# Hybrid encoder trunk on one core: the whole program scheduled on the framework's detailed timing simulator instead of its simple one

## The chip, the cores and the metric

The kernel runs on one core of one Trainium2 chip. The metric is the device time of one execution in microseconds (us). The core's engines are TensorE (PE: matmuls, with weight loads listed as PEld), VectorE (DVE), ScalarE (ACT), GpSimd (POOL) and SyncE (SP, whose queue issues all transfers of this kernel). Each engine takes its instructions from a queue of its own, and semaphores tie the queues together.

## The reference

A residual stream x of 512 positions by 1024 channels, in float32, passes one even and one odd layer and a final RMSNorm:

```python
def even_layer(x, ...):
    u = rms_norm(x, norm_g) @ w_in
    q_c, kv_c, k_r, z_b, glu_a, glu_g, z_a = jnp.split(u, ...)
    o_b = mla(q_c, kv_c, k_r, w_uq, q_g, w_ukv, kv_g, cos, sin) * jax.nn.silu(z_b)
    o_a = conformer_conv(glu_a, glu_g, conv_w, conv_b, ln_g, ln_b) * jax.nn.silu(z_a)
    return x + (jnp.concatenate([o_b, o_a], axis=-1) @ w_out).astype(x.dtype)

def odd_layer(x, ...):
    u = rms_norm(x, norm_g) @ w_in
    z_c, xbc, dt_f, dt_b, g_b, g_c, h_d, z_d = jnp.split(u, ...)
    o_c = ssd_mixer(z_c, xbc, dt_f, dt_b, ...)
    o_d = short_conv(g_b, g_c, h_d, conv_d_w) * jax.nn.silu(z_d)
    return x + (jnp.concatenate([o_c, o_d], axis=-1) @ w_out).astype(x.dtype)
```

`mla` is full attention with 16 heads over 512 positions, on low-rank queries and keys. `conformer_conv` is a gated input, a depthwise convolution of width 31, a layer norm over the channels and a swish. `ssd_mixer` is a state-space scan in chunks of 128 positions, in both directions, with 24 heads in 4 groups, behind a depthwise convolution of width 5 and followed by a gated, grouped norm. `short_conv` is a gated depthwise convolution of width 3.

## The kernel before

**Matmuls and weights.** Each float32 product is split into a high and a low part (fp32r) and made as three matmuls: high x high, high x low, low x high. A weight slab is transferred to a raw tile (two buffers), cast to `w_hi` on ScalarE (L87) and reduced to its remainder `w_lo` (L88), on VectorE for early slabs and every second one of the output projections, otherwise on GpSimd; `w_hi` and `w_lo` have three buffers each. `mm_cm` (L318) makes one tile of 128 channels by 512 positions with 24 matmuls into one bank; `mm_tm` (L345) makes four tiles with positions on the partitions. PSUM has eight banks by tag: acc 3, cv 1, sb 2, tp 2.

**Even layer.** Normed input (L405 to L407), the low-rank inputs, then eight pairs of heads. For each pair and each block of 128 queries the scores go into an sb bank (L529), VectorE takes their maximum `mx` (L531), ScalarE the exponential `p` (L533). The blocks of p are transposed on TensorE (L266) into a tp bank, copied out (L556), and multiplied with the values (L566). Scores of the block after next need the sb bank that the exponential has released. Projections (L318) for the gates and the convolution's input stand in between. In program order the width 31 convolution comes behind all eight pairs: per tile of 128 channels, ScalarE starts it in the cv bank (L470), VectorE adds 22 taps (L481), GpSimd the others on the side (L478 to L484). Behind it come the layer norm's statistics (L632 to L640, result `rs2`) and their broadcast over the partitions by a small matmul (L273, two results in the two sb banks). The output projection `oe` (L345) takes the attention's tiles, split into `o_s` pages, as its first four slabs, and calls `conformer` ahead of the fifth:

```python
def conformer():
    for ct in range(8):
        th, v, y = page("ln_th", "att"), page("ln_v", "att"), u[ct]
        V.tensor_tensor(y, y, lb[0], op=ALU.mult)                # L649
        V.tensor_tensor(y, y, lb[1], op=ALU.subtract)            # L650
        SC.activation(th, y, AF.Tanh, ...)                       # L651
        SC.activation(v, y, AF.Identity, ...)                    # L652
        V.scalar_tensor_tensor(v, th, 1.0, v, ...)               # L653
        G.tensor_tensor(oT[8 + ct], oT[8 + ct], v, op=ALU.mult)  # L654
    for o, p in zip((oh, ol), split_pages(oT[8:], None, (big("o_hi"), big("o_lo")))):
        o.extend(p)                                              # L360 o_hi, L361 o_lo
```

`split_pages` casts to `o_hi` on ScalarE (L360) and takes the remainder `o_lo` on GpSimd for each third tile, the first among them, and on VectorE for the others (L361).

**Odd layer.** For each group of heads, channel tiles are projected (L318), convolved with width 5 (ScalarE L718, four taps on VectorE L720, a tanh on ScalarE, the product on VectorE L722; the tiles are named c, c5, BT and CT) and transposed into an sb bank (L266). The scan's pairs of heads make decay factors on ScalarE and VectorE (L898 to L907, results e and f), the products within a chunk (L910, cv bank), the state's share (L862 to L868, St; L926, L931 to L936, xs), and the norm (L946 to L950). Projections of the next group's tiles are handed in between as work to fill. The output projection `oo` (L345) and the final norm end the program.

**What sets the order.** Nothing in the kernel says what stands where in a queue. The program is written as a sequence of calls, and the framework's tile context schedules it: it simulates the engines, and at each simulated moment lets an engine take, of the operations whose inputs and buffers are ready, the one that is earliest in program order. The order in which the operations were taken becomes the order of the queue. Buffers of a tag are handed out in the same walk. So the convolutions, late in program order but ready early, serve as fill on VectorE and GpSimd beside the attention pairs.

Of the kernel before, what the change touches and what calls it, by code (L numbers as in the profile page):

```python
# [1072 lines left out]
def _program(arrays, dbg=None):  # L1073
    import concourse.bacc as bacc

    nc = bacc.Bacc("TRN2", target_bir_lowering=False, num_devices=1)
    A = {n: nc.dram_tensor("in_" + n, a.shape, mybir.dt.from_np(a.dtype), kind="ExternalInput").ap()
         for n, a in arrays.items()}
    out = nc.dram_tensor("out", (S, D), F32, kind="ExternalOutput").ap()
    with tile.TileContext(nc) as tc, ExitStack() as ctx:  # L1080
        trunk(ctx, tc, A, out, dbg)
    return nc

# [8 lines left out]
```

## Time and profile before

| | us |
|---|---|
| time, median of 3 runs | 990.68 (989.94 to 990.91) |
| the profiled execution | 989.05 |
| its span in the trace | 987.2 |
| TensorE busy / VectorE busy in the span | 929.5 / 737.1 |
| ScalarE busy / GpSimd busy | 464.8 / 385.2 |
| mean granted TensorE clock | 0.983 of full speed |

The span is the time from the first to the last instruction of the profiled execution. The stages follow one another: input and low-rank projections to about 60 us, the attention pairs with the convolutions to about 400, the Conformer's tail and the output projection to about 500, the odd layer's inputs to about 600, the state-space groups to about 890, the last output projection and norm to the end. A line of a view names the source line, the engine, the operation and its tiles (result<-inputs). Idle time stands with what ended it.

### The profile page before, as it was taken

The numbers are of one execution on the slowest core, as the hardware profiler recorded it, in microseconds if no ns is written. First come the engines' busy times: TensorE is split into PE (matmuls) and PEld (weight loads), VectorE is DVE, ScalarE is ACT, GpSimd is POOL, SyncE is SP. The second block draws the span as 40 slices with busy tenths as digits, with TensorE's granted clock in tenths as the row PEclk, the third lists the DMA queues.
The fourth block names the chain that finished last, engine by engine and source line by source line (L and its number), as shares of the span: only waits on it lengthen the run. The fifth ranks groups of instructions, "written<-read, shape, count | busy, mean of one in ns | idle before, by whom it ended". The sixth has DMA issues, their size and how long they took to land. (4 is left out here: it accounts for less than half of the span.)

```text
span 987.2 us, 12582 instructions
## 1 busy us (share of the span) xinstructions
PE 929.5 (94%) x4564; PEld 754.8 (76%) x4564; DVE 737.1 (75%) x1295; ACT 464.8 (47%) x916; POOL 385.2 (39%) x272
## 2 busy tenths in 40 slices
PE   7899999999999999999999999888878988999996
PEld 7887686686786777888899987766756876787885
DVE  4799888899898998952357457899898968956205
ACT  6646444454444544543242546455456555434312
POOL 0251734526337063461143454334423443445221
PEclk9999999999999999999999999999889999999999
DMA  8313312212212126233343533432332423322222
GB/s 307 102 30 112 56 54 66 70 25 102 70 25 96 52 69 168 71 112 107 123 142 89 172 110 104 106 86 86 107 107 88 124 89 103 111 101 90 87 86 86
DMA packets 42326, 95.99 MB, mean 97 GB/s; under 512 B 12136, under 2 KB 13800, under 8 KB 42264
## 3 DMA queue, kind: packets, MB, share of 16 engines
q1 hardware_dynamic: 42264, 95.19, 31.2%
q8 instruction: 36, 0.59, 0.2%
q14 instruction: 26, 0.21, 0.1%
HBM read 90.85 MB, written 4.33 MB: 96 GB/s over the span
## 5 line engine op out<-in xcount | busy, mean ns | idle before, releaser
L88 POOL TENSOR_TENSOR w_lo<-w_raw,w_hi 128x1024 fp32r<-128x1024 f32 (+2 forms) x68 | 160.4, 2361 | 254.2 <-ACT w_hi L87 155.1
L87 ACT CAST w_hi<-w_raw 128x1024 fp32r<-128x1024 f32 (+7 forms) x142 | 135.0, 952 | 202.9 <-PE acc L318 58.7
L318 PE MATMUL acc<-xT_hi,w_hi 128*128 128x512 f32 x544 | 223.1, 412 | 2.7 <-ACT xT_hi L406 2.7
L318 PE MATMUL acc<-xT_lo,w_hi 128*128 128x512 f32 x544 | 220.9, 407 | 0.0
L88 DVE TENSOR_TENSOR w_lo<-w_raw,w_hi 128x1024 fp32r<-128x1024 f32 (+6 forms) x74 | 83.8, 1132 | 96.8 <-ACT w_hi L87 92.5
L318 PE MATMUL acc<-xT_hi,w_lo 128*128 128x512 f32 x544 | 144.7, 400 | 0.0
L481 DVE SCALAR_TENSOR_TENSOR cv<-u,pc,cv 128x497 f32<-128x497 f32 (+10 forms) x176 | 130.2, 740 | 10.0 <-ACT cv L470 7.7
L318 PEld LDWEIGHTS acc<-xT_hi,w_hi 128*128 128x128 f32 x544 | 106.0, 195 | 25.6 <-ACT xT_hi L406 2.9
L318 PEld LDWEIGHTS acc<-xT_lo,w_hi 128*128 128x128 f32 x544 | 105.6, 194 | 22.4 <-POOL xT_lo L407 0.4
L318 PEld LDWEIGHTS acc<-xT_hi,w_lo 128*128 128x128 f32 x544 | 103.3, 192 | 21.3
L479 POOL TENSOR_TENSOR side<-side 128x510 f32<-128x510 f32 (+3 forms) x56 | 78.5, 1402 | 4.7
L484 POOL TENSOR_TENSOR u<-cs,side 128x512 f32<-128x512 f32 x8 | 11.0, 1374 | 157.1 <-issue 149.9
L533 ACT ACTIVATE p<-sb,mx 128x512 f32<-128x512 f32 x64 | 43.4, 684 | 20.9 <-DVE mx L531 20.6
L904 DVE SCALAR_TENSOR_TENSOR e<-e,nacs 128x128 f32<-128x128 f32 x96 | 45.9, 520 | 9.6 <-ACT e L903 9.6
L478 POOL TENSOR_SCALAR side<-u,pc 128x510 f32<-128x510 f32 (+3 forms) x56 | 50.2, 897 | 4.7
L899 DVE SCALAR_TENSOR_TENSOR f<-cbm,dt,f 128x128 f32<-128x128 f32 x96 | 47.4, 538 | 0.4 <-ACT f L898 0.4
L531 DVE TENSOR_REDUCE mx<-sb 128x1 f32<-128x512 f32 x64 | 41.7, 685 | 3.2 <-PE sb L529 2.4
L903 ACT ACTIVATE e<-e,nacs 128x128 f32<-128x128 f32 x96 | 31.4, 391 | 22.1 <-DMA e<-acs 18.9
L720 DVE SCALAR_TENSOR_TENSOR c<-acc,pc,c 128x510 f32<-128x510 f32 (+1 forms) x48 | 35.7, 743 | 7.7 <-ACT c L718 7.4
L266 PEld LDWEIGHTS tp<-kc,p 128*128 128x128 f32 x256 | 28.9, 140 | 16.0 <-ACT pt L556 10.7
L529 PE MATMUL sb<-k_t,qk_hi 128*128 128x512 f32 (+1 forms) x128 | 39.6, 404 | 0.5 <-DVE k_t L257 0.4
L566 PE MATMUL acc<-pt,v_tm 128*64 128x512 f32 x128 | 37.6, 608 | 1.5 <-DVE pt L556 1.5
(336 smaller groups left out, 1918.5 us busy)
## 6 DMA issues: line engine op xcount, KB each, us to landing
w_raw<-in_w_cm_o SPq DMA_DIRECT2D x36, 512.0 KB, 3.5
w_raw<-in_w_cm_e SPq DMA_DIRECT2D x32, 512.0 KB, 3.6
e<-acs SPq DMA_DIRECT2D x24, 512.0 KB, 5.2
w_raw<-in_w_out_e SPq DMA_DIRECT2D x16, 512.0 KB, 3.5
w_raw<-in_w_out_o SPq DMA_DIRECT2D x16, 512.0 KB, 3.5
w_raw<-in_w_z SPq DMA_DIRECT2D x12, 384.0 KB, 3.2
xt<-in_xT SPq DMA_DIRECT2D x8, 256.0 KB, 5.2
x_t<-in_x SPq DMA_DIRECT2D x4, 512.0 KB, 6.9
```

Source lines behind the costliest of these rows:

```text
L87: nc.scalar.copy(hi, raw)
L88: eng.tensor_tensor(lo, raw, hi.bitcast(F32), op=ALU.subtract)
L318: T.matmul(a, l, r, start=n == 0, stop=n == 3 * kk - 1)
L478: G.tensor_scalar(t[:, o], ut[:, i], wt(j), 0.0, op0=ALU.mult, op1=ALU.add)
L479: G.tensor_tensor(side[:, o], side[:, o], t[:, o], op=ALU.add)
L481: V.scalar_tensor_tensor(c[:, o], ut[:, i], wt(j), c[:, o], op0=ALU.mult, op1=ALU.add)
L529: T.matmul(s, l[:, qs], r, start=n == 0, stop=n == 2)
L531: V.tensor_reduce(mx, s, axis=AX.X, op=ALU.max, negate=True)
L533: SC.activation(p, s, AF.Exp, bias=mx, accum_out=sums[:, q:q + 1])
L566: T.matmul(o[j * HD:(j + 1) * HD], v_tm[:, k, (h0 + j) * HD:(h0 + j + 1) * HD], pt, start=k == 0, stop=k == NT - 1, skip_group_check=True)
L899: V.scalar_tensor_tensor(f[:, cc], cbm[1][:, cc], dt[:, c, hb:hb + 1], f[:, cc], op0=ALU.mult, op1=ALU.add)
L904: V.scalar_tensor_tensor(e[:, cc], rb[:, 1, cc], nacs[:, c, hb:hb + 1], e[:, cc], op0=ALU.add, op1=ALU.min)
```

## The change

One argument is added where the tile context is made. The scheduler then takes its simulated moments from the framework's detailed timing simulator and no longer from the simple one:

```diff
-    with tile.TileContext(nc) as tc, ExitStack() as ctx:
+    with tile.TileContext(nc, schedule_with_timeline_sim=True) as tc, ExitStack() as ctx:
         trunk(ctx, tc, A, out, dbg)
```

The operations are the same in number and kind, and so are pools, tags and buffer counts; 370 of 1654 tiles get another buffer of their tag. On TensorE 3134 of 4278 instructions stand at another place (132 later to 51 earlier), on VectorE 1096 of 1295, on ScalarE 665 of 803, on GpSimd 80 of 274 (at most 9 places), on SP 85 of 231 (at most 7). Three places follow; a tile's number is that of its allocation.

**VectorE, from the first to the second pair of heads.** mx_1146 is the first maximum of the second pair, cv_3384 and cv_3428 are the second and third tile of the convolution, oT_1091 is the first pair's output. Before:

```order
L617 TENSOR_TENSOR oT_1091<-acc_1094,oT_1091 128x512
L481 SCALAR_TENSOR_TENSOR cv_3384<-u_735,pc_81,cv_3384 128x506
L257 TENSOR_TENSOR qk_lo_1139<-tp_1133,qk_hi_1138 96x512
L589 TENSOR_TENSOR oT_1091<-oT_1091,inv_947 128x512
L531 TENSOR_REDUCE mx_1146<-sb_1142 128x1
L531 TENSOR_REDUCE mx_1154<-sb_1150 128x1
L88 TENSOR_TENSOR w_lo_1272<-w_raw_1269,w_hi_1271 128x1024
L531 TENSOR_REDUCE mx_1162<-sb_1158 128x1
```

Now, the same maxima:

```order
L617 TENSOR_TENSOR oT_1091<-acc_1094,oT_1091 128x512
L257 TENSOR_TENSOR qk_lo_1139<-tp_1133,qk_hi_1138 96x512
L481 SCALAR_TENSOR_TENSOR cv_3428<-u_1029,pc_81,cv_3428 128x504
L589 TENSOR_TENSOR oT_1091<-oT_1091,inv_947 128x512
L481 SCALAR_TENSOR_TENSOR cv_3428<-u_1029,pc_81,cv_3428 128x505
L481 SCALAR_TENSOR_TENSOR cv_3428<-u_1029,pc_81,cv_3428 128x506
L481 SCALAR_TENSOR_TENSOR cv_3428<-u_1029,pc_81,cv_3428 128x507 x2
L481 SCALAR_TENSOR_TENSOR cv_3428<-u_1029,pc_81,cv_3428 128x506
L531 TENSOR_REDUCE mx_1146<-sb_1142 128x1
L531 TENSOR_REDUCE mx_1154<-sb_1150 128x1
```

The taps of the third tile, which stood behind the second pair before, stand ahead of its first maximum. Between the first maximum of the first pair and mx_1146 there are 39 taps, where there were 15.

**TensorE and GpSimd, the join of the Conformer.** sb_3866 and sb_3871 are the two broadcasts of the layer norm's factors (L273), acc_3882 and acc_3916 gate projections, w_hi_3992 and w_hi_4022 the third and fourth slab of the output projection, w_hi_4052 the fifth, the first that takes the Conformer's tiles. TensorE before:

```order
L318 MATMUL acc_3882<-xT_hi_435,w_lo_3729 128x512 x7
L273 MATMUL sb_3866<-kc_80,rs2_3845 128x128 x4
L273 MATMUL sb_3871<-kc_80,rs2_3845 128x128 x4
L318 MATMUL acc_3882<-xT_hi_435,w_lo_3729 128x512
L318 MATMUL acc_3916<-xT_hi_435,w_hi_3878 128x512
L318 MATMUL acc_3916<-xT_lo_436,w_hi_3878 128x512
```

TensorE now, first the broadcasts, then the start of the fifth slab:

```order
L345 MATMUL acc_3958<-w_hi_3992,o_s_3776 128x512
L345 MATMUL acc_3958<-w_hi_3992,o_s_3777 128x512
L273 MATMUL sb_3866<-kc_80,rs2_3845 128x128 x4
L273 MATMUL sb_3871<-kc_80,rs2_3845 128x128 x4
L345 MATMUL acc_3958<-w_hi_3992,o_s_3780 128x512
L345 MATMUL acc_3958<-w_hi_3992,o_s_3781 128x512
L345 MATMUL acc_3958<-w_lo_3993,o_s_3776 128x512
L345 MATMUL acc_3958<-w_lo_3993,o_s_3780 128x512
L345 MATMUL cv_3959<-w_hi_3992,o_s_3776 128x512
```

```order
L345 MATMUL cv_3959<-w_lo_4023,o_s_3784 128x512
L345 MATMUL cv_3959<-w_lo_4023,o_s_3788 128x512
L345 MATMUL acc_3956<-w_hi_4052,o_hi_4144 128x512
L345 MATMUL acc_3957<-w_hi_4052,o_hi_4144 128x512
L345 MATMUL acc_3958<-w_hi_4052,o_hi_4144 128x512
L345 MATMUL cv_3959<-w_hi_4052,o_hi_4144 128x512
L345 MATMUL acc_3956<-w_hi_4052,o_lo_4145 128x512
```

The broadcasts stood ahead of the last gate projection and of all four o_s slabs; they stand in the middle of the third of them now, 87 matmuls later, with 34 matmuls between them and the first on o_hi. On GpSimd, the difference (- before, + now) at the products L654 of the same tiles:

```order
+L88 TENSOR_TENSOR w_lo_4053<-w_raw_4050,w_hi_4052 128x1024
 L654 TENSOR_TENSOR oT_2944<-oT_2944,ln_v_4081 128x512
-L88 TENSOR_TENSOR w_lo_3993<-w_raw_3990,w_hi_3992 128x1024
 L654 TENSOR_TENSOR oT_2978<-oT_2978,ln_v_4089 128x512
+L88 TENSOR_TENSOR w_lo_4195<-w_raw_4192,w_hi_4194 128x1024
 L654 TENSOR_TENSOR oT_3202<-oT_3202,ln_v_4097 128x512
-L361 TENSOR_TENSOR o_lo_4145<-oT_2944,o_hi_4144 128x512
 L654 TENSOR_TENSOR oT_3236<-oT_3236,ln_v_4105 128x512
 L654 TENSOR_TENSOR oT_3723<-oT_3723,ln_v_4113 128x512
 L654 TENSOR_TENSOR oT_3757<-oT_3757,ln_v_4121 128x512
-L88 TENSOR_TENSOR w_lo_4053<-w_raw_4050,w_hi_4052 128x1024
+L361 TENSOR_TENSOR o_lo_4145<-oT_2944,o_hi_4144 128x512
```

The remainder o_lo of the first of the Conformer's tiles stood behind three products, and stands behind six and another weight remainder now.

**TensorE, a channel tile of the odd layer.** c5_7240 is a channel tile, acc_7293 and acc_7502 are the projections of the next ones. Before:

```order
L318 MATMUL acc_7293<-xT_lo_4568,w_hi_7243 128x512
L318 MATMUL acc_7293<-xT_hi_4567,w_hi_7243 128x512
L318 MATMUL acc_7293<-xT_lo_4568,w_hi_7243 128x512
L318 MATMUL acc_7293<-xT_hi_4567,w_lo_7244 128x512 x8
L849 MATMUL tp_7332<-CT_7038,BT_7079 128x128 x3
L266 MATMUL sb_7280<-kc_80,c5_7240 128x128 x4
L849 MATMUL tp_7332<-CT_7038,BT_7079 128x128
```

Now:

```order
L318 MATMUL acc_7502<-xT_hi_4567,w_hi_7289 128x512
L318 MATMUL acc_7502<-xT_lo_4568,w_hi_7289 128x512
L318 MATMUL acc_7502<-xT_hi_4567,w_lo_7290 128x512 x5
L266 MATMUL sb_7280<-kc_80,c5_7240 128x128 x4
L318 MATMUL acc_7502<-xT_hi_4567,w_lo_7290 128x512 x3
```

The transpose of the tile stood behind the projection into acc_7293; it stands behind most of the following one too. Between the end of a tile's own projection and its transpose the queue of this stage held 27 to 44 matmuls, and holds 45 to 91 now.

## The prediction

> **What bounds the kernel now.** I read the page first, then the busy times by 25 us stretches, then TensorE's waits, and last the timeline at the places where the order moves.
>
> ```profile
> span 987.2 us, 12582 instructions
> ...
> PE 929.5 (94%) x4564; PEld 754.8 (76%) x4564; DVE 737.1 (75%) x1295; ACT 464.8 (47%) x916; POOL 385.2 (39%) x272
> ```
>
> TensorE is busy for 929.5 of 987.2 us, so all that any order could win is 57.7 us of idle time and whatever the clock takes. Whether VectorE is near it is a question of the stage:
>
> ```profile
> 425.00:450.00 25.00, 25.00 (x112) 20.70 (x111) 11.83 (x13) 7.79 (x12) 11.38 (x7) 1.00 0.44 147
> 625.00:650.00 25.00, 20.55 (x94) 16.75 (x93) 22.92 (x43) 10.49 (x22) 7.82 (x5) 0.86 0.39 105
> ```
>
> The columns are PE, PEld, DVE, ACT, POOL, the granted clock and DMA. From 425 to 600 us PE is full and VectorE half idle: no order gains there, and a moderate one loses nothing. In the SSD stage (600 to 890) PE has holes, VectorE is nearly full, and the clock falls to 0.86. The attention stage lies between:
>
> ```profile
> 85.00:128.40 43.40, 43.20 (x201) 31.88 (x200) 40.36 (x58) 23.48 (x50) 17.71 (x17) 1.00 0.34 72
> ```
>
> Here both engines are full: PE is idle for 0.2 us and DVE for 3.0 us of 43.4. Two full engines that hand work to each other stay full only if their queues are interleaved as the chip runs them. So this stage can lose from a new order and gain next to nothing; the SSD stage is where there is something to win.
>
> **The change part by part.** No operation is added or taken out; each engine runs its instructions in the order of its queue. Four places matter.
>
> *Attention, first to second head pair.* Rows for the convolution taps and weight remainders on VectorE in that stretch:
>
> ```profile
> L481 DVE SCALAR_TENSOR_TENSOR cv<-u,pc,cv 128x501 f32<-128x501 f32 (+9 forms) x15 | 11.1, 739 | 0.2
> L88 DVE TENSOR_TENSOR w_lo<-w_raw,w_hi 128x1024 fp32r<-128x1024 f32 (+1 forms) x5 | 5.7, 1143 | 0.6 <-PE acc L318 0.6
> ```
>
> Between the maxima mx_875 and mx_1211 (85.0 to 128.4 us) VectorE's queue holds 19 taps before and 48 now, and two w_lo fewer: 29 x 0.739 - 2 x 1.143 = 19.1 us more, 40.4 + 19.1 = 59.5 us of DVE work. TensorE holds 199 matmuls between the scores of the same two maxima before and 204 now, five small ones more, some 1.1 us: 43.2 + 1.1 = 44.3 us. TensorE can't run past a maximum, since the next scores need the sb bank (two of them) and the transposes need the exponentials. So it falls behind by 59.5 - 44.3 = 15.2 us at mx_1211; the last transposes that need it stand behind 18 projection matmuls (18 x 0.227 = 4.1 us of cover), one exponential comes on top (0.7): 15.2 + 0.7 - 4.1 = 11.8. The 0.227 is the distance of matmul starts in the join rows below, the 0.7 this row:
>
> ```profile
> 117.75 0.69 ACT L533 ACTIVATE p<-sb,mx 128x512 f32<-128x512 f32 x1
> ```
>
> I find no second growth of the lag: the taps that came early are missing later. But PE was full there, so a hole isn't paid back. I take **+12 us**. Lower end +5: TensorE's waits from 50 to 420 us before are those below and some smaller, about 7 us in all, and VectorE's later slack could remove them. Upper end +17: the whole 15.2 and a clock drop (1.7, below) behind the holes.
>
> ```profile
> PE acc L345 <- ACT q_tm L503: 4.0, 3, 1.5
> PE acc L566 <- DVE pt L556: 1.5, 2, 1.0
> ```
>
> *Join of the Conformer.* The rows of 399 to 433 us, then the moments:
>
> ```profile
> L654 POOL TENSOR_TENSOR oT<-oT,ln_v 128x512 f32<-128x512 f32 x8 | 12.3, 1536 | 17.7 <-DVE ln_v L653 17.7
> L653 DVE SCALAR_TENSOR_TENSOR ln_v<-ln_th,ln_v 128x512 f32<-128x512 f32 x8 | 9.0, 1139 | 0.0
> L651 ACT ACTIVATE ln_th<-u,lg 128x512 f32<-128x512 f32 x8 | 6.5, 809 | 4.1 <-DVE u L650 4.0
> L652 ACT ACTIVATE ln_v<-u,lg 128x512 f32<-128x512 f32 x8 | 6.4, 803 | 0.0
> L88 POOL TENSOR_TENSOR w_lo<-w_raw,w_hi 128x1024 fp32r<-128x1024 f32 x2 | 5.3, 2633 | 0.0
> L650 DVE TENSOR_TENSOR u<-u,sb 128x512 f32<-128x512 f32 x8 | 5.3, 677 | 0.0
> L649 DVE TENSOR_TENSOR u<-u,sb 128x512 f32<-128x512 f32 x8 | 5.2, 678 | 1.1 <-PE sb L273 1.1
> L361 POOL TENSOR_TENSOR o_lo<-oT,o_hi 128x512 fp32r<-128x512 f32 x3 | 4.8, 1591 | 0.0
> L87 ACT CAST w_hi<-w_raw 128x1024 fp32r<-128x1024 f32 x5 | 5.1, 1043 | 0.0
> L88 DVE TENSOR_TENSOR w_lo<-w_raw,w_hi 128x1024 fp32r<-128x1024 f32 x2 | 2.4, 1216 | 0.0
> ```
>
> ```profile
> 399.51 2.05 PE L273 MATMUL sb<-kc,rs 128*128 128x128 f32 x16
> ...
> 427.95 1.74 POOL L361 TENSOR_TENSOR o_lo<-oT,o_hi 128x512 fp32r<-128x512 f32 x1
> ...
> 428.87 0.39 PE L345 MATMUL acc<-w_hi,o_hi 128*128 128x512 f32 x1
> ...
> 429.10 0.39 PE L345 MATMUL acc<-w_hi,o_lo 128*128 128x512 f32 x1
> ```
>
> Before, the broadcast of the layer norm's factors (L273) ran at 399.5, and the first matmul on the Conformer's tiles at 428.9: 29 us, which PE filled with projections and the o_s half. Now L273 stands 87 matmuls further back, inside the second last o_s slab, and only 34 matmuls lie between it and the first o_hi: 34 x 0.227 = 7.7 us, with the second broadcast (1.0) and four o_hi matmuls (0.9) a cover of 9.6 us. Behind it: VectorE does eight L649 (5.2), eight L650 (5.3) and a w_lo (1.2) before the first L653 (1.1): 12.8 us. GpSimd then does two L654, a w_lo and four L654 ahead of o_lo: 6 x 1.54 + 2.63 + 1.59 = 13.5 us, so o_lo lands 26.3 us behind L273; at some 1.3 us for an L654 (an estimate for less crowding, against the mean of 1.54) it is 24.5. ScalarE is no later: from the first L650 (5.9 us) it has 13 activations of 0.81 and a cast (1.0) ahead of o_hi, 17.4 us. TensorE waits 24.5 - 9.6 = 14.9 to 16.7 us. I take **+15 us**, with +10 (VectorE and GpSimd undisturbed by each other, DVE ahead) and +19 (16.7 and a clock drop) as ends.
>
> *SSD stage.*
>
> ```profile
> 600.00:890.00 290.00, 256.85 (x1254) 206.89 (x1252) 246.98 (x477) 152.58 (x340) 112.72 (x62) 0.95 0.33 100
> ```
>
> ```profile
> PE cv L910 <- DVE f L907: 9.1, 6, 2.6
> PE sb L266 <- DVE c L722: 9.0, 4, 3.2
> PE sb L266 <- DVE BT L722: 6.4, 2, 3.3
> PE tp L266 <- DVE xs L950: 4.1, 2, 2.4
> ```
>
> PE idles for 290 - 256.9 = 33 us, and a clock of 0.95 takes another 290 x 0.05 = 14. In the fence on waits, the columns are total, times, longest. The clock falls where PE has stood still for about 2 us or more:
>
> ```profile
> 629.00:631.59 2.59, 0.00 (x1) 0.01 (x1) 2.59 (x7) 1.09 (x2) 0.00 (x0) 1.00 0.00 0
> 632.40:635.80 3.40, 3.40 (x13) 2.83 (x13) 2.06 (x5) 2.25 (x6) 0.58 (x1) 0.50 0.66 193
> ```
>
> A hole of 2.59 us is followed by 3.4 us at 0.50, which is 1.7 us of work lost. [...]
>
> Between the end of a channel tile's projection and the transpose (L266 into sb) of that tile the queue held 27 to 44 matmuls before (fourteen tiles) and holds 45 to 91 now, 17 to 59 more: 3.9 to 13 us of further cover, against longest waits of 3.3. L910 stands 19 places later in the median and its L907 eight earlier on VectorE. So the waits on L722 (15.4 us) and about half of those on L907 (4.5) should go, and with them five of the eight clock drops (14 / 1.7; 5 x 1.7 = 8.5): 28 us. Against it stands VectorE: it is busy for 247 of the 290 us, so the stage can't fall by more than 43, and its own queue was shuffled too (L868, L919, L931 and L934 later by 14 to 37 places in the median), so new waits on these arise. I take **-18 us**, with -34 and -5 as ends; the last is one drop in three and nothing else.
>
> *The rest.* Start: the order of the first casts changes by one or two 1 us steps either way, 0 +- 2. SP's transfers move by at most 7 places, with DMA at a third of its capacity, covered by the three buffers of each weight: 0; a slab without that cover would cost its landing time, 3.5 us. From 425 to 600 us: 0, VectorE half idle.
>
> ```profile
> w_raw<-in_w_cm_o SPq DMA_DIRECT2D x36, 512.0 KB, 3.5
> ```
>
> **Rivals.**
>
> *The SSD stage comes down to VectorE's own work.* If VectorE never waits there, the gain is 34 us rather than 18, while the two stalls cost what they should: 12 + 15 - 34 = -7, that is 984. It decides from an SSD gain of 29 us on. For it: 247 of 290, and cover longer than any wait. Against: VectorE has 43 us of waits of its own there, and a queue in simulated order gives new ones. **0.22**.
>
> *It cancels.* The SSD gain lies within 2 us of the stalls: 991. **0.07**.
>
> *VectorE's shuffle eats the SSD gain.* A wait on a late L868 or L931 takes the place of that on L722, only 5 us are won: 12 + 15 - 5 = +22, 1013. For it: the moves of L868 to L934 just named, each a step that TensorE waits for in the end. **0.21**.
>
> *Order doesn't count.* Excluded as a whole: 3134 of TensorE's 4278 instructions stand elsewhere.
>
> **How the numbers follow.** The forecast, **0.50**, is 12 + 15 - 18 = +9 us. The profiled execution took 989.05 (span 987.2); with +9 its span would be 996 and its time 998. It lies 1.6 below the median of 990.68, so that the median becomes 990.68 + 9 = 999.7, rounded 1000; its own range, with one of the two stalls at an end (+2 to +14), is 993 to 1005. For 8 in 10 the range reaches from the first rival's 984 less its unknown of 2 to the third's 1013 plus a stall at its upper end (5): **982 to 1018**. About 0.2%, 2 us, is what a measurement of this kernel can tell from no change (its three runs lie within 1 us). Faster 0.22, same 0.07, slower 0.50 + 0.21 = 0.71.
>
> **What would show it.** Right: TensorE waits of 10 us or more in all on mx, p or exponentials between 90 and 150 us; one hole of 10 us or more ahead of the first L345 on o_hi or o_lo, released by L654, L360 or L361; SSD waits of L266 on L722 under 5 us, and a mean clock in that stage of 0.97 or more. Wrong: if VectorE's taps fill time in which it idled without delaying mx_1146; if the broadcast L273 finds more cover than 9.6 us; if the SSD stage stays at 285 us or more, or goes below 256.

## The result and the profile after

The changed kernel takes 1096.66 us (median of 4 runs, 1090.65 to 1098.51) against 990.31 us for the kernel before, run beside it: a ratio of 1.1075, 95% interval 1.1046 to 1.1105, 106 us slower. The prediction had 1000, at most 1018. The profiled execution has a span of 1095.7 us, 108.5 more than before.

The page after. TensorE's clock fell from 0.983 to 0.938, and its busy time rose by 52 us for the same 4564 matmuls; VectorE's is unchanged:

```profile
span 1095.7 us, 12605 instructions
...
PE 981.4 (90%) x4564; PEld 778.9 (71%) x4564; DVE 741.4 (68%) x1295; ACT 462.7 (42%) x916; POOL 380.1 (35%) x272
```

To see where the time went, I cut both traces at moments when TensorE had done the same work: each matmul of either queue gets the distance of starts that its kind has in the trace before, and the cuts are set at equal sums. The matmul counts of the stretches show that the cuts match. The columns are length, then busy us (and count) of PE, PEld, DVE, ACT, POOL, the granted clock, DMA share and GB/s. Before, attention with the convolutions, the odd layer's inputs, and the SSD stage:

```profile
54.00:410.00 356.00, 348.57 (x1734) 266.86 (x1733) 324.01 (x489) 171.81 (x336) 156.06 (x141) 1.00 0.26 71
450.00:596.00 146.00, 145.64 (x743) 129.55 (x742) 66.64 (x145) 56.84 (x99) 54.41 (x26) 1.00 0.38 122
596.00:900.00 304.00, 270.85 (x1321) 218.43 (x1320) 259.43 (x493) 161.11 (x353) 122.01 (x68) 0.96 0.32 97
```

After, the same three and, second, the join of the Conformer with the first output slabs, which took 40 us before:

```profile
57.90:496.20 438.30, 391.37 (x1723) 280.43 (x1723) 308.00 (x464) 168.70 (x330) 144.01 (x140) 0.93 0.19 59
496.20:554.80 58.60, 43.31 (x188) 35.15 (x187) 39.70 (x51) 24.92 (x35) 26.00 (x14) 0.85 0.21 72
554.80:711.40 156.60, 148.38 (x740) 133.24 (x740) 69.13 (x146) 55.64 (x98) 53.99 (x26) 0.97 0.36 113
711.40:1007.00 295.60, 271.64 (x1314) 221.29 (x1313) 258.09 (x476) 156.29 (x349) 127.41 (x68) 0.94 0.33 102
```

| stage | before, us | after, us | difference | predicted |
|---|---|---|---|---|
| start | 54.0 | 57.9 | +4 | 0 |
| attention and convolutions | 356.0 | 438.3 | +82 | +12 |
| join of the Conformer | 40 | 58.6 | +18 | +15 |
| the odd layer's inputs | 146 | 156.6 | +11 | 0 |
| SSD groups | 304 | 295.6 | -8 | -18 |
| output projection and norm | | | 0 | 0 |

The attention stage holds three quarters of the loss. TensorE's idle time there rose from 7.4 to 46.9 us and the clock fell from 1.00 to 0.93, which is another 30 us; the last 12 us lie in time that the profile counts as busy. What TensorE waited for from 85 to 510 us (total, times, longest):

```profile
PE tp L266 <- ACT p L533: 24.3, 25, 2.2
PE sb L529 <- ACT p L533: 10.5, 11, 1.3
```

Waits on the exponentials p, which the trace before doesn't list at all. The timeline shows how they arise. Before, in the fifth pair, the scores of two blocks (L529) and then a run of projections (L318), in which maximum and exponential have time:

```profile
242.96 0.67 PE L529 MATMUL sb<-k_t,qk_hi 96*128 96x512 f32 x2
243.46 0.40 PE L529 MATMUL sb<-k_t,qk_lo 96*128 96x512 f32 x1
243.70 0.62 PE L529 MATMUL sb<-k_t,qk_hi 96*128 96x512 f32 x2
244.16 0.39 PE L529 MATMUL sb<-k_t,qk_lo 96*128 96x512 f32 x1
244.39 0.40 PE L318 MATMUL acc<-xT_lo,w_hi 128*128 128x512 f32 x1
```

After, in the same pair, with the idle time before an instruction and its releaser in brackets:

```profile
299.69 0.71 PE L529 MATMUL sb<-k_t,qk_hi 96*128 96x512 f32 x2
300.24 0.39 PE L529 MATMUL sb<-k_t,qk_lo 96*128 96x512 f32 x1
300.47 0.27 PE L266 MATMUL tp<-kc,p 128*128 128x128 f32 x1
301.98 0.33 PE L266 MATMUL tp<-kc,p 128*128 128x128 f32 x1 [1.23 <-ACT p L533]
302.64 0.33 PE L266 MATMUL tp<-kc,p 128*128 128x128 f32 x1 [0.34 <-ACT p L533]
303.11 1.22 PE L529 MATMUL sb<-k_t,qk_hi 128*128 128x512 f32 x4
304.14 1.04 PE L529 MATMUL sb<-k_t,qk_lo 128*128 128x512 f32 x2
306.35 1.22 PE L529 MATMUL sb<-k_t,qk_hi 128*128 128x512 f32 x2 [1.17 <-ACT p L533]
```

From the third block of a pair on, scores follow scores, and the first transposes of p stand among them. Counted in the queues: between the third and the eighth score block of a pair stood 19 to 23 projection matmuls before and no transpose of p; now 0 and five, in all eight pairs. The holes of about 1.2 us look like the chain of score, maximum (0.69 us) and exponential (0.69) with nothing beside it, and the clock drops with them; what of this is cause, the experiments try.

The join, after: one hole ahead of the first o_hi, one ahead of the first o_lo.

```profile
522.96 1.65 PE L345 MATMUL acc<-w_hi,o_hi 128*128 128x512 f32 x3 [7.70 <-ACT o_hi L360]
...
532.63 0.80 PE L345 MATMUL acc<-w_hi,o_lo 128*128 128x512 f32 x1 [7.59 <-POOL o_lo L361]
```

### The profile page after: what moved, and what is told of

Same layout as the page of the kernel before. It is cut to its first block, busy times and chain, and to the rows that moved or that the text cites. A ratio compares the mean times of both kernels' runs of the same rounds, so it can differ in the third digit from the quotient of the medians.

```text
span 1095.7 us, 12605 instructions
## 1 busy us (share of the span) xinstructions
PE 981.4 (90%) x4564; PEld 778.9 (71%) x4564; DVE 741.4 (68%) x1295; ACT 462.7 (42%) x916; POOL 380.1 (35%) x272
## 5 line engine op out<-in xcount | busy, mean ns | idle before, releaser
L88 POOL TENSOR_TENSOR w_lo<-w_raw,w_hi 128x1024 fp32r<-128x1024 f32 (+2 forms) x68 | 166.4, 2449 | 280.7 <-ACT w_hi L87 244.2
L318 PE MATMUL acc<-xT_hi,w_hi 128*128 128x512 f32 x544 | 225.3, 415 | 6.4 <-DVE BT L720 2.9
L318 PE MATMUL acc<-xT_lo,w_hi 128*128 128x512 f32 x544 | 223.4, 411 | 4.0 <-DVE xT_lo L407 3.6
L318 PE MATMUL acc<-xT_hi,w_lo 128*128 128x512 f32 x544 | 149.2, 406 | 0.0
L318 PEld LDWEIGHTS acc<-xT_hi,w_hi 128*128 128x128 f32 x544 | 107.1, 197 | 39.8 <-issue 7.3
L318 PEld LDWEIGHTS acc<-xT_lo,w_hi 128*128 128x128 f32 x544 | 107.1, 197 | 28.8 <-DVE xT_lo L407 4.3
L318 PEld LDWEIGHTS acc<-xT_hi,w_lo 128*128 128x128 f32 x544 | 101.5, 192 | 24.4 <-issue 3.5
L479 POOL TENSOR_TENSOR side<-side 128x510 f32<-128x510 f32 (+3 forms) x56 | 74.3, 1327 | 4.7
L266 PE MATMUL tp<-kc,p 128*128 128x128 f32 x256 | 49.8, 293 | 24.5 <-ACT p L533 24.3
L266 PEld LDWEIGHTS tp<-kc,p 128*128 128x128 f32 x256 | 33.6, 147 | 41.7 <-ACT p L533 32.9
L529 PE MATMUL sb<-k_t,qk_hi 128*128 128x512 f32 (+1 forms) x128 | 49.1, 491 | 11.6 <-ACT p L533 10.5
L903 ACT ACTIVATE e<-e,nacs 128x128 f32<-128x128 f32 x96 | 30.7, 389 | 52.7 <-DMA e<-acs 49.7
L904 DVE SCALAR_TENSOR_TENSOR e<-e,nacs 128x128 f32<-128x128 f32 x96 | 41.7, 484 | 16.0 <-ACT e L903 16.0
L566 PE MATMUL acc<-pt,v_tm 128*64 128x512 f32 x128 | 49.1, 652 | 0.7 <-DVE pt L556 0.7
L478 POOL TENSOR_SCALAR side<-u,pc 128x510 f32<-128x510 f32 (+3 forms) x56 | 43.0, 767 | 4.7
```

Source lines behind the costliest of these rows:

```text
L88: eng.tensor_tensor(lo, raw, hi.bitcast(F32), op=ALU.subtract)
L266: T.transpose(tp[:rows, j * P:(j + 1) * P], b, ident)
L318: T.matmul(a, l, r, start=n == 0, stop=n == 3 * kk - 1)
L479: G.tensor_tensor(side[:, o], side[:, o], t[:, o], op=ALU.add)
L529: T.matmul(s, l[:, qs], r, start=n == 0, stop=n == 2)
L566: T.matmul(o[j * HD:(j + 1) * HD], v_tm[:, k, (h0 + j) * HD:(h0 + j + 1) * HD], pt, start=k == 0, stop=k == NT - 1, skip_group_check=True)
```

## The experiments

Theory A: the attention stage loses because scores and transposes stand on TensorE without projections between them. Theory B, the prediction's: it loses because VectorE's taps stand ahead of the maxima. All experiments use one addition. It takes lists of instructions of one engine, by their names in program order, and ties each to the one before it in the list, on its own queue and without a semaphore, so that the scheduler must queue them in that order:

```diff
+def pinned(tc, nc, chains):
+    by = {i.name: i for i in nc.cur_bb.bb.instructions}
+    info = mybir.DependencyInfo(mybir.DependencyClass.NoSync, mybir.DependencyReason.DATA)
+    for chain in chains:
+        names = ["I-%d" % n for n in chain]
+        for a, b in zip(names, names[1:]):
+            tc.add_manual_dep(by[b], a, info, reason="order")
...
         trunk(ctx, tc, A, out, dbg)
+        pinned(tc, nc, CHAINS)
```

In the diffs below the lists have words for names. Every kernel computes the whole reference. A run on the changed kernel is set against 1096.66 us, either by the times or by the difference of the two ratios. Ratios are to the kernel before on the same chip (986.6 to 988.4 us), with 95% intervals.

**Order or buffers.** Detailed simulator, all five queues in the order before.

```diff
     with tile.TileContext(nc, schedule_with_timeline_sim=True) as tc, ExitStack() as ctx:
+CHAINS = [before[e] for e in (PE, DVE, ACT, POOL, SP)]
```

> The changed kernel, scheduled on the detailed simulator, with all five queues held in the order of the kernel before. If order alone makes the difference, the time before comes back, 983 to 993. If other buffers and waits that the detailed simulator gives out have a part, it stays 5 us or more above.

987.59 us, ratio 0.9985 (0.9956 to 1.0013). Order is the whole cause: with the order held, the other simulator costs nothing. Which tiles had other buffers in this run is not on record, so it says nothing of buffers that only another order hands out; the kernels below that take the changed order on the simple simulator bear on that.

**TensorE's order in the attention stage.** On the changed kernel:

```diff
+CHAINS = [before[PE] from the first scores to L273]
```

> The changed kernel with one thing taken back: TensorE's 1466 instructions from the first scores to the broadcast L273 stand in the order of the kernel before (19 to 23 projection matmuls between the third and the eighth score block of each pair again, where the changed kernel has 0, and no transpose of p among the scores). VectorE, ScalarE and GpSimd are left to the detailed simulator; 32 taps stand ahead of mx_1211 (19 before, 48 changed). Theory A, uncovered scores: of the 82 us that the attention stage loses, 70 to 82 come back, time 1015 to 1028. Theory B, the prediction's, taps ahead of the maxima: the taps stay early by 13, so some 65 us or more of the loss stay, 1080 or above.

1027.80 us, ratio 1.0417 (1.0383 to 1.0451): 69 us come back (65 by the ratios). That is A's edge, 1028; B falls as the main cause. The taps moved with it, from 48 to 32 ahead of mx_1211, so the next run tries these. The waits on p are gone, 0.4 us are listed where it was 34.8; from 80 to 435 us TensorE now waits a little for the next queries:

```profile
PE sb L529 <- ACT qk_hi L256: 6.6, 7, 2.2
...
PE sb L529 <- ACT p L533: 0.4, 2, 0.3
```

By equal work the stage still loses 19 us, 13 of them by the third pair, where the taps are early.

**VectorE's order there.** On the changed kernel:

```diff
+CHAINS = [before[DVE] from mx_875 to L640]
```

> The changed kernel with VectorE's 429 instructions from mx_875 to L640 in the order of the kernel before (19 taps ahead of mx_1211), TensorE left to the detailed simulator: 0 projection matmuls between the third and the eighth score block of a pair, five transposes of p among the scores. Theory A: at most the 12 us of the first handover come back, 1083 to 1097. Theory B: the whole stage comes back, 1015 to 1028.

1109.75 us, ratio 1.1248 (1.1182 to 1.1313): 13 us worse than the changed kernel, or 17 by the ratios. With taps in their old places and scores still bunched nothing comes back, which neither theory had. That VectorE's old interleaving is in the wrong place for TensorE's new order is a guess that no run tried.

**Both.**

```diff
+CHAINS = [before[PE] from the first scores to L273, before[DVE] from mx_875 to L640]
```

> The changed kernel with TensorE's 1466 and VectorE's 429 instructions of the attention stage in the order of the kernel before. TensorE's alone left 19 us of the 82 in that stage. If these are the early taps (24 and 32 of them ahead of mx_1146 and mx_1211), 13 to 19 us come back against the run with TensorE's order alone (1027.8), 1009 to 1015. Rival: they come from ScalarE's casts and the weights, and less than 5 come back, 1023 or more.

1005.02 us, ratio 1.0161 (1.0118 to 1.0204): 23 us less than with TensorE's order alone (25 by the ratios), more than the 13 to 19 expected. By equal work the stage loses 1 us. So its 82 us are TensorE's order first, and early taps behind it.

**The two the other way round.** On the kernel before, simple simulator, TensorE's attention order as changed:

```diff
     with tile.TileContext(nc) as tc, ExitStack() as ctx:
+CHAINS = [after[PE] for the instructions from the first scores to L273]
```

> The kernel before, simple simulator, with TensorE's instructions of the attention stage alone in the changed kernel's order (scores bunched, five transposes among them), join and odd layer as before. Theory A: the attention stage's loss alone appears, 1055 to 1075. Theory B: 35 taps ahead of mx_1211 instead of 19 or 48, so 12 us at most, 990 to 1003.

1063.63 us, ratio 1.0780 (1.0719 to 1.0841): +77 us, 73 of them in this stage by equal work, and the waits of the changed kernel are there. No other engine was tied, but the scheduler answered with 35 taps ahead of mx_1211 instead of 19, so a part may be theirs:

```profile
PE tp L266 <- ACT p L533: 22.3, 25, 2.1
PE sb L529 <- ACT p L533: 11.0, 10, 1.4
```

By equal work, cut from 85 us on, it loses 8 to 12 us in every stretch of 40 us of TensorE's work, from the first pair to the last; early taps cost only at the first pairs, as the next run shows. And the taps alone, ahead of the maxima of the second pair, TensorE's order untouched:

```diff
+CHAINS = [before[PE] from the first scores to L273, after[DVE] from mx_875 to mx_1211, L481 and L531 only]
```

> The kernel before, simple simulator, TensorE's order wholly as before; only the taps L481 move: 49 stand ahead of mx_1211 (19 before, 48 changed). It tries the prediction's first term by itself. As predicted, two full queues against each other: +12 us, +5 to +17. Rival: VectorE's 3 us of slack and its earlier arrival take most of it, 0 to +4.

1014.96 us, ratio 1.0260 (1.0228 to 1.0292): +26 us, above the prediction's range for the term. The waits from 70 to 420 us:

```profile
PE sb L529 <- ACT p L533: 17.4, 3, 14.8
PE sb L529 <- ACT qk_hi L256: 3.7, 1, 3.7
```

The stretch of these pairs, 88.2 us before by equal work, with its columns as above:

```profile
54.50:169.00 114.50, 92.36 (x435) 71.76 (x433) 100.69 (x147) 47.74 (x92) 56.75 (x59) 0.93 0.17 45
```

One hole of 14.8 us, where the prediction's sum of the two queues had 15.2; around it idle time of 114.5 - 92.4 - 14.8 = 7 us, and a clock of 0.93, up to another 8 us, which the sum left out. Behind 169 us nothing more is lost. The two parts don't add: 73 us and 26 alone, 82 together.

**Transposes or banks.** On the changed kernel, the transposes of p behind the pair's last scores:

```diff
+CHAINS = [[last L529 of the pair, t] for each pair, for each of its transposes t of p]
```

> The changed kernel with the transposes of p of each pair held behind the last score matmul of that pair on TensorE; the scores stay bunched (0 projections between the third and the eighth block). Theory A in two parts: if the transposes at the head of the queue are the cost (24.3 us of waits on p in 25 places and their clock drops), 40 to 60 us come back, 1037 to 1057; if the two sb banks set the pace of bunched scores, the waits of L529 on p take their place and 0 to 20 come back, 1077 to 1097.

1089.88 us, ratio 1.1046 (1.0992 to 1.1101): 3 us by the ratios, 7 by the times come back, as in the second reading. The waits from 85 to 510 us move, but not as it had them: those of L529 on p stay at 10.6 us, and new ones on the next pair's queries `qk_hi` appear:

```profile
PE sb L529 <- ACT qk_hi L256: 23.1, 8, 4.1
PE sb L529 <- ACT p L533: 10.6, 11, 1.3
PE acc L345 <- ACT q_tm L503: 8.0, 3, 3.8
PE tp L266 <- ACT p L533: 5.2, 9, 1.1
```

The transposes are not the cost: bunched scores wait for banks and queries wherever the transposes stand. What else TensorE's old order gives back is the projections between the blocks; that they are what counts follows by exclusion, since no run put them back alone.

**The join.** On the changed kernel:

```diff
+CHAINS = [before[PE] from the last gates to the fifth output slab,
+          before[e] around L649 to L654, L360, L361 for e in (DVE, ACT, POOL)]
```

> The changed kernel with the Conformer's join alone in the order of the kernel before: TensorE's 177 instructions from the last gate projections over the broadcast L273 to the fifth output slab, and the 33, 28 and 13 of VectorE, ScalarE and GpSimd around L649 to L654, L360 and L361. If the prediction's join is right (fresh holes of 7.7 and 7.6 us ahead of o_hi and o_lo, 18.5 us between equal points of TensorE's work), 16 to 20 us come back against the changed kernel's 1096.7. Rival: late statistics (rs2) hold the earlier broadcast up, and half or more of the hole moves ahead of L273: 0 to 9 us come back.

1068.87 us, one run: 28 us come back (25 against the kernel before on the same chip, 988.16), more than expected. By equal work the join loses nothing any more (18 before), which is the 16 to 20 expected. The other 8 us come from the attention stage, whose order was not touched: TensorE idles as long there (45.9 us, 46.9 in the changed kernel, from 85 to 395 us of the kernel before by equal work), but stands at half clock for 41 us where it was 61. The last section shows how equal holes can cost unequal clock, and the four runs of the changed kernel differ by 8 us too; so in this one run it is taken for luck and not for an effect of the join. The two runs with TensorE's attention order bear on the mechanism too: there 64 matmuls stood between L273 and o_hi instead of 34, o_lo landed as late (26.8 us behind L273), and by equal work the join lost 11 us. In the profile TensorE is full there again:

```profile
480.00:520.00 40.00, 40.00 (x178) 33.12 (x177) 33.08 (x33) 23.71 (x33) 26.80 (x15) 1.00 0.33 105
```

**The odd layer.** On the kernel before, from 490 us on, four engines as changed:

```diff
+CHAINS = [after[e] for the instructions from 490 us on, for e in (PE, DVE, ACT, POOL)]
```

> The kernel before with all four engines' instructions of the odd layer (from 490 us on) in the changed kernel's order. If order alone makes the difference there, the layer's inputs lose 9 to 11 us and the SSD stage gains 7 to 9: 0 to +4 us against the kernel before. Rival: the changed kernel's other buffers and its late start shaped these waits: below -4 or above +8.

994.87 us, ratio 1.0061 (1.0037 to 1.0085), some 6 us slower: within -4 to +8, beyond the narrower expectation. By equal work the inputs lose 9 us and the SSD stage gains 6, close to the changed kernel's 11 and 8. So this order costs and gains on the simple simulator as well.

**The SSD stage by itself,** in six cuts, all on the kernel before:

```diff
+CHAINS = [after[e] from 600 us on, for e in (PE, DVE, ACT, POOL)]             # first
+CHAINS = [after[PE] from 600 us on]                                          # second
+CHAINS = [[projection that precedes t in after, t] for each t of L266 into sb]  # third
+CHAINS = [after[e] from 600 to 850 us, for e in (PE, DVE, ACT, POOL)]         # fourth
+CHAINS = [after[PE] from 600 to 850 us]                                      # fifth
+CHAINS = [after[PE] from 600 to 790 us]                                      # sixth
```

> The kernel before with all four engines' instructions from 600 us on in the changed kernel's order; attention, join and the odd layer's inputs as before. Order as the cause: the SSD stage's gain without the rest, -6 to -10 us against the kernel before, faster than both. The prediction's -18 for the stage would show here in full if the stalls upstream had hidden it. Rival: nothing is left of the gain, -3 to +3.

984.83 us, ratio 0.9961 (0.9940 to 0.9983): -4 us. Between the two expectations, but a gain.

> The kernel before with TensorE's 1438 instructions from 600 us on in the changed kernel's order, the other engines left to the simple simulator. If the gain is TensorE's cover ahead of the channel tiles' transposes, it comes without VectorE's shuffle too, -6 to -18 us. Rival: VectorE's new order is what pays (decays ahead, St later), and TensorE's alone gives -2 to +6.

984.07 us, ratio 0.9957 (0.9938 to 0.9977): -4 us. VectorE's shuffle neither pays nor costs beside TensorE's order.

> The kernel before with one thing of the changed order: the 56 transposes of the SSD stage's channel tiles (L266 into sb) stand behind the projection matmul that precedes them in the changed order; all else is left to the simple simulator. If the cover ahead of these transposes is what pays (15.4 us of waits on L722 and their clock drops in the kernel before), -8 to -20 us. Rival: the waits move on to L910, L862 or L926, which VectorE feeds later still, -3 to +3.

992.46 us, ratio 1.0048 (1.0026 to 1.0070): 5 us slower, beyond the rival's range too. The transposes' cover alone is worth nothing; the waits move on. SSD stage, 590 to 900 us:

```profile
PE cv L910 <- DVE f L907: 16.2, 9, 4.5
PE tp L266 <- DVE xs L950: 6.1, 2, 4.3
PE sb L266 <- DVE c L722: 5.7, 1, 5.7
```

> The kernel before with all four engines in the changed kernel's order from 600 to 850 us alone; the last group's end and its handover to the output projection as before. If the stage's missing gain is given back at that handover (10 us between equal points of TensorE's work behind 857 us), -8 to -15 us. Rival: it is given back within the stage, by new waits on VectorE and by clock drops, so cutting the end off changes nothing, -2 to -6.

982.18 us, ratio 0.9942 (0.9920 to 0.9963): -5 us, the lowest time of this study, faster than the kernels before and after; its interval overlaps those of the two cuts above that gain.

> The kernel before with TensorE alone in the changed kernel's order from 600 to 850 us. If the handover takes the gain, -8 to -12 us; if new waits within the stage do, -2 to -6.

984.98 us, ratio 0.9969 (0.9950 to 0.9988): -3 us.

> The kernel before with TensorE alone in the changed kernel's order from 600 to 790 us, two and a half of the four groups. If each group gains alike and the end loses, -4 to -8 us; if the gain sits in the first group alone (-11 us by 640 us in the run with TensorE's order to the end), -8 to -11; if later groups give it back whatever stands at the end, -2 to +2.

988.54 us, ratio 1.0000 (0.9978 to 1.0021): no gain. Single runs of the kernel before on this chip lie between 983 and 993 us, so the gains of 3 to 5 us rest on medians of 5 to 10 runs.

Leaving out the handover at the end changes the gain by a microsecond or two at most, which is within the intervals, so it is not there that the rest of it goes. It goes within the stage. In the first cut, 600 to 890 us, against the row of the same window that the prediction shows:

```profile
600.00:890.00 290.00, 264.11 (x1274) 215.68 (x1274) 252.35 (x469) 149.84 (x336) 123.92 (x64) 0.93 0.33 102
```

TensorE idles for 25.9 us where it idled for 33.2, but the clock is 0.93 where it was 0.95: 7 us less idle, some 6 or 7 more lost to the clock. In this window it still makes 20 matmuls more. The waits that are left are many and small:

```profile
PE tp L862 <- DVE St L868: 4.4, 2, 2.4
PE tp L266 <- ACT zg L956: 3.5, 1, 3.5
PE cv L910 <- DVE f L907: 3.5, 1, 3.5
...
PE sb L266 <- DVE c L722: 0.5, 1, 0.5
```

## Why the prediction was wrong, point by point

**Slower, by the wrong amount.** The sign was right and the time outside its range. Of five terms one was off by 70 us.

**Attention, +12.** As an effect of the taps alone the first handover was described rightly: maxima late behind the taps, a hole of 14.8 us where the two queues gave 15.2. Its size was still too small by half, since the sum discounted cover that didn't show and left the clock out (+26 in the run with the taps alone). In the changed kernel itself this hole doesn't stand: from 90 to 150 us the waits on p are 8.7 us in all, 2.2 the longest, for TensorE was already held up by its own order. The step that failed is another: "I find no second growth of the lag: the taps that came early are missing later." That is true of the taps, and the run shows it: behind 169 us it loses nothing more. But from it I concluded that the stage held nothing more, and so looked at one handover of eight. The scores of every pair had lost the 19 to 23 projections between their blocks, and TensorE's new order cost 8 to 12 us in each 40 us of its work. The order showed it: scores and transposes of p without a projection between them, rows that I had read for what stands ahead of mx_1211 and not for what a block's own latency needs. A sum of two queues' work sees a queue that is too full; it doesn't see a chain that goes to and fro between engines with nothing beside it. "An order can gain next to nothing here" was right, and "+17" as the upper end was no bound at all.

**Join, +15.** Right in mechanism and size: predicted were 26.3 us from L273 to o_lo and a wait of 14.9 to 16.7. L273 ran at 505.6; o_lo landed at 532.6, 27 us later, and the two holes are 7.70 and 7.59, 15.3 us. The clock, 0.85 in this stretch, made 18 of it. It came as two holes and not as the one of 10 us or more that was named as a sign. A sum was off: with 1.3 us for an L654 it gives 24.8 us and a wait of 15.2, not 24.5 and 14.9. The rows from 505 to 540 us show that GpSimd's products are no quicker than in the crowd before:

```profile
L654 POOL TENSOR_TENSOR oT<-oT,ln_v 128x512 f32<-128x512 f32 x8 | 13.4, 1703 | 12.4 <-DVE ln_v L653 12.4
L653 DVE SCALAR_TENSOR_TENSOR ln_v<-ln_th,ln_v 128x512 f32<-128x512 f32 x8 | 12.5, 1624 | 0.0
```

Means of 1703 and 1624 ns, against 1536 and 1139 before: bunched, the two run beside each other all the time, and the estimate of 1.3 us for less crowding went the wrong way. The one L653 with no GpSimd work beside it took 0.70 us, the six wholly beside it 1.74 us or more.

**SSD, -18.** The waits on L722 went as forecast, 15.4 to 0.5 us, and those on L907 from 9.1 to 4.1. But "with them five of the eight clock drops" failed: the clock didn't rise at all (0.96 to 0.94). New waits on St, gt, xs and zg took the place of some of the old, as the third rival had it, and small holes cost clock too: from 897.60 to 901.00 us after the change the longest is 1.33 us, TensorE is busy for 2.07 of 3.40 us, and the next 3.40 us stand at 0.57. The gain is 8 us in the changed kernel and 3 to 5 by itself. Cover ahead of the channel tiles' transposes, taken alone, even costs 5 us; of the parts tried on TensorE alone, its order from 600 to 850 us or to the end pays, and to 790 us does not. The prediction had taken 10 us off its 28 for VectorE without a sum behind it, and that was too little.

**The two zeros.** The start lost 4 and the odd layer's inputs 11. The stretch from 425 to 600 us was called safe because VectorE is half idle there; but TensorE depends there on weights that ScalarE casts in its own queue's order, and one slab came late: its cast starts at 662.99 us, behind eight exponentials (L903), the first of which waited for a transfer until 659.22 us. From 600 to 700 us after:

```profile
PE sb L345 <- ACT w_hi L87: 5.2, 1, 5.2
PE acc L266 <- DVE xn L305: 2.3, 1, 2.3
```

Slack on another engine is no cover when the order ahead of one input changes. The start's 4 us were not followed up.

## What to carry to other kernels

When an order changes, follow every hand-over that repeats, in all its repetitions: count what the waiting engine now has between the step it sends and the step it waits for, and set that against the latency of the chain, not against the sum of the other queue. Bound a term from above by what the stage would take if its chains ran one after the other with nothing beside them. And an order can be tried piece by piece: tying some instructions to another schedule's order shows within one run which piece pays, and here found a kernel 0.6% faster than the one before (0.4% to 0.8%).

## What the runs showed of the hardware

The clock dropped here without a hole of 2 us. In the fifth pair after the change, stretches of 3.4 us:

```profile
300.80:304.20 3.40, 1.75 (x7) 1.20 (x8) 2.12 (x4) 2.26 (x6) 0.00 (x0) 0.99 0.48 154
304.20:307.60 3.40, 2.23 (x6) 1.31 (x5) 1.29 (x2) 1.45 (x4) 0.00 (x0) 0.50 0.00 0
307.60:311.00 3.40, 2.14 (x7) 1.14 (x6) 2.08 (x3) 1.45 (x4) 0.00 (x0) 0.50 0.00 0
311.00:314.40 3.40, 3.40 (x9) 2.72 (x10) 1.06 (x3) 1.55 (x4) 1.03 (x2) 0.50 0.14 1
314.40:317.80 3.40, 3.40 (x17) 2.74 (x16) 0.20 (x1) 1.18 (x2) 3.13 (x4) 1.00 0.02 5
```

The longest hole up to 304 us is 1.23 us, yet the stretch in which TensorE was busy for 1.75 of 3.40 us is followed by three at 0.50, and the clock came back behind a full one (311.0 to 314.4). In the two traces, before and after the change, what told the drops apart was the busy time of a whole stretch, not its longest hole. The changes in their clock records, from the first drop to the last, stand at multiples of 3.41 us from each other (after the change, half clock from 304.14 us for 10.24 us, from 348.51 for 6.83, from 403.12 for 3.41). With the traces cut at that distance, all 31 stretches at full clock in which TensorE was busy for less than 1.8 us (9 before, 22 after) were followed by half clock, and none with more than 2.2 us was; of the 16 between these, two were, with 2.08 and 2.11 us. Where a hole lay in these stretches made a difference too: in the kernel before, the hole of 1.86 us from 643.68 us on left its stretch 1.55 us of work and cost a drop; the longer one of 2.36 us from 678.84 us on lay across two stretches, with 2.06 and 2.40 us of work, and cost none. The prediction's "about 2 us or more" of standing still was thus no limit. The busy times were read off the traces; no run varied them alone.
